# A hybrid decoder layer on one core: gate chunks of 512 columns and step sizes computed as [head, token]

## The chip, the core and the metric

The kernel runs on one core of one Trainium2 chip. The core has a matrix engine (TensorE, PE in the profile), a vector engine (VectorE, DVE), a scalar engine (ScalarE, ACT), a general engine (GpSimd, POOL) and SyncE (SP), whose queue issues all of this kernel's transfers. Each engine works through its own instructions in the order in which they stand; semaphores order them between engines. PE reads operands from the on-chip memory SBUF and writes results into PSUM; ACT and DVE read PSUM and write SBUF. The metric is the device time of one execution in microseconds (us); smaller is better.

## What is computed

One decoder layer over 256 tokens of width 1024 in float32: a SwiGLU feed-forward layer, a token mixer, a cross-attention and a second feed-forward layer, each with RMS norms. The change lies in the mixer. Its input projection gives `q`, `k`, `v` of an attention branch, `z`, `xbc` and `dt` of a state-space branch (SSD), and the logits of two gates that merge the branches:

```python
h = _rmsnorm(x, mix_pre_g)
q, k, v, z, xbc, dt_raw, gate_logits = jnp.split(h @ w_in, cuts, axis=-1)
...
dt = jax.nn.softplus(dt_raw + ssd_dt_bias)          # 32 heads, one step size per head and token
a = -jnp.exp(ssd_A_log)
y = _ssd_chunked(xh * dt[..., None], a * dt, B, C)
...
g_attn, g_ssd = jnp.split(jax.nn.sigmoid(gate_logits + b_gate), 2, axis=-1)
mixed = (g_attn * attn_out + g_ssd * ssd_out) @ w_mix_out
```

In `w_in` the 32 columns of `dt_raw` stand directly ahead of the 2048 columns of `gate_logits`.

## The kernel before

Tokens lie in two tiles of 128 (`t` = 0, 1), the width of 1024 in eight slices `k` of 128. The normalised input of the mixer is kept transposed as `hT`, a high part and a low part, both in fp32r. Every weight is loaded into a `raw` buffer (six of them) as a tile of 128 x 1024 (one slice or more), and then split: ACT copies the high part (`whi_...`), DVE subtracts it from the raw values to get the low part (`wlo_...`). There are nine slots for each part. A product is three matmuls (`mm3`, L175 to L178): high by high, high by low, low by high. The helper class `Engine` records ACT's and DVE's instructions, so they all carry the line L57 (L55 with a raised priority); they are told apart by tile names.

`proj_B` (L337) gives a product as [token, column]: the 128 tokens of tile `t` are stationary and up to 512 weight columns move. `proj_A` (L319) gives it as [column, token]: 128 weight columns are stationary and 256 tokens move. `proj_A2` (from L327, in the feed-forward layers) puts the high and the low part of `hT` side by side, so that one matmul with 512 moving columns does high by high and high by low, and a second one with 256 does low by high.

The gates and dt share one projection of 2080 columns, cut into five chunks of `GCH` = 416 (L35). `gate_w` (L652) loads and splits the weights of a chunk, four tiles of 832 columns each. `gate_chunk` (L655) does, for one token tile, 24 matmuls of 416 columns; DVE then adds the bias into `sig` (kept in two tiles, `sig0` and `sig1`) and ACT takes the tanh. In chunk 0 the first 32 columns are dt: DVE adds `dtb` and writes `dtr`.

The order of the work around it is written out by hand, and a scheduler then places each engine's instructions by that order and by priorities. Behind the last product of `v` (`da_v`, L572) come five small transposes (`cw_ps`), then gate chunk 0 for both token tiles, then a softplus of `dtr` by some twenty small DVE operations and one ACT exponential (`sp_e`, `sp_r`, `sp_u`, `sp_pl`, from L683), which end in `dt` and `adt`. Then the loop of L995 runs the attention: `q0 k0 q1 k1 q2 k2 o0 q3 o1 k3 g1 o2 g2 o3`, where `q` and `k` are projections, `o` output products, and `g1`, `g2` gate chunks. `k0` also starts `cumulate` (L703), which needs `adt`. The softmax work of the attention runs in chains that advance at fixed points (`tick`) of the projections. Behind the SSD groups come gate chunks 3 and 4 (L1024) and the merge, in which DVE multiplies and adds `sig` with the branch results (L1033 to L1038).

The splits of `q0`, `k0` and chunk 0 are told not to stand ahead of the evacuation of `hT`'s second half (`last`, L586, L677).

Of the kernel before, what the change touches and what calls it, by code (L numbers as in the profile page):

```python
# [8 lines left out]
F32 = mybir.dt.float32  # L9
# [4 lines left out]
ALU = mybir.AluOpType  # L14
# [4 lines left out]
P = 128  # L19
S = 256  # L20
NT = S // P
D = 1024
KD = D // P
# [7 lines left out]
SSD_HEADS = 32  # L31
HG = 8
HP = 64
C_Q, C_K, C_V, C_Z, C_X, C_B, C_C, C_DT = 0, 1024, 2048, 3072, 5120, 7168, 7680, 8192
GCH = 416  # L35
NSLOT = 9
WARM = 18
NRAW = 6
# [31 lines left out]
def tile_hybrid_layer(ctx: ExitStack, tc: tile.TileContext, a: dict, out: bass.AP):  # L70
    nc = tc.nc
    V, A, T, G, SY = Engine(tc, nc.vector), Engine(tc, nc.scalar), nc.tensor, nc.gpsimd, nc.sync

    cp = ctx.enter_context(tc.tile_pool(name="const", bufs=1))
    sp = ctx.enter_context(tc.tile_pool(name="small", bufs=3))
# [5 lines left out]
    def mm_bank(name):  # L81
        return ps.tile([P, 512], F32, tag="mm", bufs=2, name=name)

    def ch_bank(name):
        return ps.tile([P, 512], F32, tag="ch", bufs=2, name=name)
# [4 lines left out]
    def pool(name, bufs=1):  # L90
        return tc.tile_pool(name=name, bufs=bufs, reuse_waits="tile")
# [13 lines left out]
    def start(key, gen):  # L105
        chains[key] = gen
        active.append(key)
        step(key)
# [6 lines left out]
    def tick():  # L115
        for key in list(active):
            step(key)
# [5 lines left out]
    ident = cp.tile([P, P], F32, name="ident")  # L123
# [4 lines left out]
    def issue_after(after, i):  # L128
        return nullcontext() if after is None else tc.issue_after(after[i].ins)

    def wslot(z, name, xtra=None):
        pl, bufs, tag = (wp, NSLOT, f"w{z}") if xtra is None else xtra[z == "lo"]
        return pl.tile([P, 1024], F32R, tag=tag, bufs=bufs, name=f"w{z}_{name}")

    def wraw(name):
        return wp.tile([P, 1024], F32, tag="raw", bufs=NRAW, name=f"raw_{name}")
# [38 lines left out]
    def mm3(o, lh, ll, rh, rl, start, stop):  # L175
        T.matmul(o, lh, rh, start=start, stop=False)  # L176
        T.matmul(o, lh, rl, start=False, stop=False)  # L177
        T.matmul(o, ll, rh, start=False, stop=stop)  # L178
# [33 lines left out]
    def split_evac(bank, hi, lo, scale=1.0):  # L212
        if scale == 1.0:
            return (A.copy(hi, bank),
                    V.tensor_tensor(out=lo, in0=bank, in1=hi.bitcast(F32), op=ALU.subtract))
        return (A.activation(hi, bank, AF.Copy, scale=scale),
                V.scalar_tensor_tensor(out=lo, in0=bank, scalar=scale, in1=hi.bitcast(F32),
                                       op0=ALU.mult, op1=ALU.subtract))
# [15 lines left out]
    def hT_tiles(name):  # L234
        return parts(hp_.tile([P, KD, 2, S], F32R, tag="hT", name=f"hT_{name}"))
# [101 lines left out]
    def proj_B(w, hT, t, ks, width, bank, k0=0, first=True, last=True):  # L337
        for k in ks:
            mm3(bank, hT[0][:, k, t * P:(t + 1) * P], hT[1][:, k, t * P:(t + 1) * P], *w(k - k0, 0, width),
                first and k == ks[0], last and k == ks[-1])  # L340
            if width > 256 and k % 4 == 3 or k == KD - 1:
                tick()
# [17 lines left out]
    def cols(ap, c0, n):  # L360
        return ap[:, c0:c0 + n]
# [122 lines left out]
    mp = ctx.enter_context(tc.tile_pool(name="mix", bufs=1))  # L484
# [4 lines left out]
    w_in = a["w_in"][0]  # L489
# [62 lines left out]
    with pool("ffn1") as fp:  # L552
        steps = ffn(fp, hT1, a["ffn1_post_g"][0], w_gu, a["ffn1_w_down"][0], "f1", ws, second_tile, nrm, memory)
        hT, xns = None, []
        for t, acc_t, g_bc in steps:
            if t == 0:
                hT = hT_tiles("mx")
# [27 lines left out]
    last = []  # L585
# [4 lines left out]
    last = last[0]  # L590
# [13 lines left out]
    dtb = mp.tile([P, SSD_HEADS], F32, name="dtb")  # L604
# [35 lines left out]

    dtr = mp.tile([P, NT, SSD_HEADS], F32, name="dtr")
    b_gate = a["b_gate"][0]
    G0 = GCH - 32
    sig0 = mp.tile([P, NT, G0], F32, name="sig0")
    gctx = ExitStack()
    gpool = gctx.enter_context(tc.tile_pool(name="gates", bufs=1, side="right", reuse_waits="tile"))
    sig1 = gpool.tile([P, NT, 2 * D - G0], F32, name="sig1")

    def sig(t, c0, c1):
        return sig0[:, t, c0:c1] if c1 <= G0 else sig1[:, t, c0 - G0:c1 - G0]  # L650

    def gate_w(j, after=None):  # L652
        return Weights([cols(w_in, C_DT + j * GCH, GCH)], KD, GCH, f"gt{j}", after)

    def gate_chunk(w, j, t, bg):  # L655
        bank = mm_bank(f"gt{j}{t}")
        proj_B(w, hT, t, range(KD), GCH, bank[:, :GCH])
        g0 = max(0, j * GCH - 32)
        o = 32 if j == 0 else 0
        n = GCH - o  # L660
        if j == 0:
            V.tensor_tensor(out=dtr[:, t, :], in0=bank[:, :32], in1=dtb, op=ALU.add)
        sg = sig(t, g0, g0 + n)
        V.tensor_tensor(out=sg, in0=bank[:, o:GCH], in1=bg[:, :n], op=ALU.add)
        A.activation(sg, sg, AF.Tanh, scale=0.5)

    def gate_bias(j):
        g0 = max(0, j * GCH - 32)
        n = GCH - (32 if j == 0 else 0)
        bg = sp.tile([P, GCH], F32, tag="bg", bufs=1, name=f"bg{j}")  # L670
        with issue_after(marks["f1"], 0):
            SY.dma_start(out=bg[:, :n], in_=b_gate[g0:g0 + n].partition_broadcast(P))
        return bg


    w_g0, bg0 = gate_w(0, last), gate_bias(0)
    for t in range(NT):  # L677
        gate_chunk(w_g0, 0, t, bg0)


    W = NT * SSD_HEADS
# [16 lines left out]
    dt = mp.tile([P, NT, SSD_HEADS], F32, name="dt")  # L698
# [146 lines left out]
    def ssd_bc(dp_, g):  # L845
        wbc = Weights([cols(w_in, C_B + g * P, P), cols(w_in, C_C + g * P, P)], KD, 256, f"bc{g}")
        bcT = dp_.tile([P, 2, S], F32, tag="bcT", name=f"bcT{g}", bufs=2)
        conv(dp_, proj_A(wbc, hT, f"bc{g}"), (16 + g, 20 + g), bcT, f"b{g}")
        return bcT
# [112 lines left out]
    def ssd_ws(g):  # L962
        return [Weights([a["w_branch_ssd"][0, g * 512 + i * 256:g * 512 + (i + 1) * 256, :]], 2, D, f"ws{g}{i}")
                for i in range(2)]

    def ssd_out(g, ws, t):
        while (g, t) not in ydone:
            step(("s", g))
        y = ydone[g, t]
        for c in range(2):  # L970
            for i in range(2):
                acc_rows(sacc, ws[i], y[0], y[1], 2 * i, t, c, g == 0 and i == 0, g == 3 and i == 1)
            tick()
# [18 lines left out]
        chain_a(j)  # L992

    units = dict(q=q, k=k, g=gates, o=da_out)
    for u in "q0 k0 q1 k1 q2 k2 o0 q3 o1 k3 g1 o2 g2 o3".split():  # L995
        units[u[0]](int(u[1]))
    cs, cs_d, ecs = finish("cs")
    for t in range(NT):
        for c0, c1 in ((0, G0), (G0, 512), (512, D)):
            V.scalar_tensor_tensor(out=sig(t, c0, c1), in0=sig(t, c0, c1), scalar=1.0,  # L1000
                                   in1=acc[t][c0 // 512][:, c0 % 512:c0 % 512 + c1 - c0], op0=ALU.add, op1=ALU.mult)
    ap_ctx.close()
# [3 lines left out]
    with pool("ssd") as dp_:  # L1006
        def out_units(g):
            ws = ssd_ws(g)
            for t in range(NT):
                ssd_out(g, ws, t)  # L1010

        for g in range(4):
            bcT = ssd_bc(dp_, g)
            xsT = dp_.tile([P, 4, S], F32, tag="xsT", name=f"xsT{g}", bufs=2)
            for i in range(2):
                ssd_xs(dp_, g, i, xsT)
            w = Weights([cols(w_in, C_Z + g * 512, 512)], KD, 512, f"z{g}")
            sz = dp_.tile([P, NT, 512], F32, tag="sz", name=f"sz{g}", bufs=2)
            for t in range(NT):
                ssd_z(g, t, w, sz)  # L1020
            if g > 0:
                out_units(g - 1)
            start(("s", g), ssd_chain(dp_, g, xsT, bcT, sz))
        for j in (3, 4):  # L1024
            w, bg = gate_w(j), gate_bias(j)
            for t in range(NT):
                gate_chunk(w, j, t, bg)
        mT = hT_tiles("mg")
        ws = ssd_ws(3)
        for t in range(NT):  # L1030
            ssd_out(3, ws, t)
            with ahead(400):
                for c in range(2):  # L1033
                    mg = sig(t, D + c * 512, D + (c + 1) * 512)
                    V.scalar_tensor_tensor(out=mg, in0=mg, scalar=1.0, in1=sacc[t][c], op0=ALU.add, op1=ALU.mult)
                    for c0, c1 in ((0, G0), (G0, 512)) if c == 0 else ((512, D),):
                        mg = sig(t, D + c0, D + c1)
                        V.tensor_tensor(out=mg, in0=mg, in1=sig(t, c0, c1), op=ALU.add)  # L1038
                transpose_split(sig(t, D, 2 * D), mT[0], mT[1], t, KD, "mg", scale=0.5)

    nctx = ExitStack()
# [61 lines left out]
    hT = hT_tiles("xa")  # L1103
# [67 lines left out]
    for t in range(NT):  # L1171
# [12 lines left out]
        with ahead(400):  # L1184
            post_norm(nrm, acc[t], g_po, t, 1.0, "xa")
            xn, last = norm_tile(nrm, x_sb[:, t, :], g_pr, t, "f2", scale_on=(V, A)[t])
# [40 lines left out]
```

## Time and profile before

| | before |
|---|---|
| runs shown | 871.56, 872.61 and 1729.69 us, median 872.61 |
| profiled execution: its time | 872.02 us |
| profiled execution: span of the instructions | 870.3 us |
| mean granted TensorE clock | 0.997 of full speed |
| busy: PE, DVE, ACT | 857.5, 622.5, 500.9 us |
| chain that ended last, share of PE | 94% |

The profile is of one execution. A timeline row gives the start in us from the span's start, the time of the instruction or of a run of equal ones, the engine, the line of the kernel, the operation, output tile <- input tiles, shapes, and the count; a bracket at its end names idle time ahead of it. PE's matmuls are pipelined: one starts before the one ahead of it has ended, so their pace is read from the starts.

### The profile page before, as it was taken

The page shows a single profiled execution, that of the slowest core. Times are in us where ns is not written, and L with a number is a line of the kernel's source. Part 1 is how long each engine was busy: PE and PEld are TensorE (multiplying, and loading weights), DVE is VectorE, ACT ScalarE, POOL GpSimd, SP SyncE. Part 2 cuts the span into 40 slices and gives each one's busy share as a digit, 9 for nine tenths or more (in the row PEclk, how much of TensorE's full clock was granted, in tenths as well). Part 3 has the DMA queues.
Part 4 walks back from the last instruction along what each step waited for, and adds up shares of the span by engine and source line. Part 5 has one row for each costly group of instructions (what it writes and reads, how often), then busy time and mean ns, then how long its engine had stood idle before and what let it go on. Part 6 is the DMA issues. An engine that isn't in the chain of part 4 may idle for free.

```text
span 870.3 us, 13275 instructions
## 1 busy us (share of the span) xinstructions
PE 857.5 (99%) x4966; PEld 752.6 (86%) x4966; DVE 622.5 (72%) x1064; ACT 500.9 (58%) x867; POOL 3.7 (0%) x14
## 2 busy tenths in 40 slices
PE   8999999999999999999999999999999999999996
PEld 5888888888999999998989888899998788888885
DVE  6876556768778677897987968797574975556653
ACT  7756555645666565966775734466453754555540
POOL 0000000000000000000000000000000000000000
PEclk9999999999999999999999999999999999999998
DMA  8877667635854267656463456577452386566601
GB/s 289 286 259 248 196 200 247 203 103 160 291 145 126 88 193 252 230 152 230 144 229 139 143 177 208 179 227 253 163 181 64 120 270 214 177 201 186 191 22 49
DMA packets 117653, 161.78 MB, mean 186 GB/s; under 512 B 6452, under 2 KB 93396, under 8 KB 117076
## 3 DMA queue, kind: packets, MB, share of 16 engines
q1 hardware_dynamic: 117588, 160.93, 58.0%
q8 instruction: 39, 0.64, 0.3%
q14 instruction: 26, 0.21, 0.1%
HBM read 158.78 MB, written 2.13 MB: 185 GB/s over the span
## 4 chain that ended last, share of the span: by engine, by line
PE 94%; DVE 2%; ACT 2%; DMA 1%; issue 1%; SPq 0%; DVEq 0%; ACTq 0%
PE u_f L331 8%; PE s_f L331 8%; PE acc_f L176 5%; PE acc_f L177 5%; PE acc_f L178 5%; PE u_f L333 4%; PE s_f L333 4%; PE pA_xs L176 2%; PE pA_xs L178 2%; PE pA_xs L177 2%; PE z L176 2%; PE z L178 2%; PE z L177 2%; PE gt L176 2%; PE gt L177 2%; PE yb L915 2%
## 5 line engine op out<-in xcount | busy, mean ns | idle before, releaser
L331 PE MATMUL s_f<-hT_f,whi_f1g 128*128 128x512 f32 x160 | 40.3, 393 | 0.0
L331 PE MATMUL u_f<-hT_f,whi_f1u 128*128 128x512 f32 x160 | 40.1, 392 | 0.0
L176 PE MATMUL pA_xs<-hT_mx,whi_xs 128*128 128x256 f32 x128 | 38.8, 303 | 0.0
L57 DVE TENSOR_TENSOR wlo_f2d<-raw_f2d,whi_f2d 128x1024 fp32r<-128x1024 f32 x22 | 26.8, 1220 | 13.5 <-PE u_f L333 10.4
L178 PE MATMUL pA_xs<-hT_mx,wlo_xs 128*128 128x256 f32 x128 | 36.2, 283 | 0.0
L177 PE MATMUL pA_xs<-hT_mx,whi_xs 128*128 128x256 f32 x128 | 36.2, 283 | 0.0
L331 PE MATMUL u_f<-hT_f,whi_f2u 128*128 128x512 f32 x144 | 36.1, 392 | 0.0
L331 PE MATMUL s_f<-hT_f,whi_f2g 128*128 128x512 f32 x144 | 35.9, 391 | 0.0
L176 PE MATMUL acc_f<-whi_f1d,hh_f 128*128 128x512 f32 x88 | 35.0, 398 | 0.0
L177 PE MATMUL acc_f<-wlo_f1d,hh_f 128*128 128x512 f32 x88 | 34.9, 396 | 0.0
L178 PE MATMUL acc_f<-whi_f1d,hl_f 128*128 128x512 f32 x88 | 34.8, 396 | 0.0
L176 PE MATMUL acc_f<-whi_f2d,hh_f 128*128 128x512 f32 x88 | 34.3, 390 | 0.0
L177 PE MATMUL acc_f<-wlo_f2d,hh_f 128*128 128x512 f32 x88 | 34.3, 390 | 0.0
L178 PE MATMUL acc_f<-whi_f2d,hl_f 128*128 128x512 f32 x88 | 34.2, 389 | 0.0
L331 PEld LDWEIGHTS s_f<-hT_f,whi_f1g 128*128 128x128 f32 x160 | 29.2, 188 | 5.6
L57 DVE TENSOR_TENSOR wlo_f1d<-raw_f1d,whi_f1d 128x1024 fp32r<-128x1024 f32 x22 | 26.8, 1220 | 10.1 <-PE u_f L333 7.5
L331 PEld LDWEIGHTS u_f<-hT_f,whi_f1u 128*128 128x128 f32 x160 | 28.8, 189 | 5.2
L57 DVE TENSOR_TENSOR wlo_f1g<-raw_f1g,whi_f1g 128x1024 fp32r<-128x1024 f32 x20 | 24.3, 1218 | 11.3 <-ACT whi_f1g L57 11.3
L57 DVE TENSOR_TENSOR wlo_f2g<-raw_f2g,whi_f2g 128x1024 fp32r<-128x1024 f32 x18 | 21.9, 1221 | 13.5 <-ACT whi_f2g L57 12.6
L331 PEld LDWEIGHTS s_f<-hT_f,whi_f2g 128*128 128x128 f32 x144 | 26.3, 188 | 5.0
L57 DVE TENSOR_TENSOR wlo_f2u<-raw_f2u,whi_f2u 128x1024 fp32r<-128x1024 f32 x18 | 22.0, 1220 | 11.9 <-PE s_f L333 8.9
L331 PEld LDWEIGHTS u_f<-hT_f,whi_f2u 128*128 128x128 f32 x144 | 25.9, 189 | 4.6
(496 smaller groups left out, 2808.4 us busy)
## 6 DMA issues: line engine op xcount, KB each, us to landing
raw_f1d<-in_ffn_w_down_dram SPq DMA_DIRECT2D x22, 512.0 KB, 4.5
raw_f2d<-in_ffn_w_down_dram SPq DMA_DIRECT2D x22, 512.0 KB, 4.3
raw_f1g<-in_ffn_w_gu_dram SPq DMA_DIRECT2D x20, 512.0 KB, 5.8
raw_f1u<-in_ffn_w_gu_dram SPq DMA_DIRECT2D x20, 512.0 KB, 5.2
raw_f2g<-in_ffn_w_gu_dram SPq DMA_DIRECT2D x18, 512.0 KB, 4.6
raw_f2u<-in_ffn_w_gu_dram SPq DMA_DIRECT2D x18, 512.0 KB, 4.1
raw_gt<-in_w_in_dram SPq DMA_DIRECT2D x20, 416.0 KB, 4.0
raw_xs<-in_w_in_dram SPq DMA_DIRECT2D x16, 512.0 KB, 5.0
```

The source lines that it names most:

```text
L57: return fn(*args, **kwargs)
L176: T.matmul(o, lh, rh, start=start, stop=False)
L177: T.matmul(o, lh, rl, start=False, stop=False)
L178: T.matmul(o, ll, rh, start=False, stop=stop)
L331: T.matmul(bank, w(k, f * P, (f + 1) * P)[0], hT[2][:, k, :], start=k == 0, stop=False)
L333: T.matmul(bank[:, S:], w(k, f * P, (f + 1) * P)[1], hT[0][:, k, :], start=False, stop=k == KD - 1)
L915: T.matmul(yb[:, h * HP:(h + 1) * HP], M[:, h, :], xdt[:, h, :], start=True, stop=True)
```

## The change

The 32 dt columns leave the gate projection. The gates are cut into four chunks of 512 columns, numbered 0 to 3; a weight tile of a chunk then has 1024 columns in place of 832, and there are 16 in place of 20. No gate chunk stands ahead of `q0` any more: chunks 0 and 1 take the places of 1 and 2 in the loop, chunks 2 and 3 those of 3 and 4 behind the SSD. `sig0` and `sig1` become one tile, and the merge's additions at the cut fall away.

dt is computed apart, ahead of `q0`. Its weights (1024 x 32) come in one load of eight pieces of 32 columns (128 bytes) per partition, and are split into `whi_dt` and `wlo_dt` (256 columns). Eight matmuls with 512 moving columns (both parts of `hT`) and eight with 256 give [head, token] in one bank; ACT copies one half to `dT`, DVE adds the other, PE turns `dT` in two transposes, and DVE adds `dtb` into `dtr` for both token tiles at once. The softplus that follows is the same.

```diff
-GCH = 416
...
-    sig0 = mp.tile([P, NT, G0], F32, name="sig0")
...
     def gate_chunk(w, j, t, bg):
         bank = mm_bank(f"gt{j}{t}")
-        proj_B(w, hT, t, range(KD), GCH, bank[:, :GCH])
...
-        if j == 0:
-            V.tensor_tensor(out=dtr[:, t, :], in0=bank[:, :32], in1=dtb, op=ALU.add)
...
+        proj_B(w, hT, t, range(KD), 512, bank)
+        sg = sig(t, j * 512, (j + 1) * 512)
+        V.tensor_tensor(out=sg, in0=bank, in1=bg, op=ALU.add)
         A.activation(sg, sg, AF.Tanh, scale=0.5)
...
-    w_g0, bg0 = gate_w(0, last), gate_bias(0)
+    dt_raw = wraw("dt")[:, :KD * SSD_HEADS].rearrange("p (k f) -> p k f", k=KD)
+    SY.dma_start(out=dt_raw, in_=cols(w_in, C_DT, SSD_HEADS).rearrange("(k p) f -> p k f", p=P))
+    dt_w = [wslot(z, "dt")[:, :KD * SSD_HEADS].rearrange("p (k f) -> p k f", k=KD) for z in ("hi", "lo")]
+    split_evac(dt_raw, *dt_w)
+    db = mm_bank("dtT")
+    for k in range(KD):
+        T.matmul(db[:SSD_HEADS], dt_w[0][:, k, :], hT[2][:, k, :], start=k == 0, stop=False)
+    for k in range(KD):
+        T.matmul(db[:SSD_HEADS, S:], dt_w[1][:, k, :], hT[0][:, k, :], start=False, stop=k == KD - 1)
+    dT = wraw("dT")[:SSD_HEADS, :S]
+    A.copy(dT, db[:SSD_HEADS, S:])
+    V.tensor_tensor(out=dT, in0=db[:SSD_HEADS, :S], in1=dT, op=ALU.add)
+    tb = ch_bank("dtt")
     for t in range(NT):
-        gate_chunk(w_g0, 0, t, bg0)
+        T.transpose(tb[:, t * SSD_HEADS:(t + 1) * SSD_HEADS], dT[:, t * P:(t + 1) * P], ident[:SSD_HEADS, :SSD_HEADS])
+    V.tensor_tensor(out=dtr, in0=tb[:, :NT * SSD_HEADS].rearrange("p (t h) -> p t h", t=NT),
+                    in1=dtb.unsqueeze(1).to_broadcast([P, NT, SSD_HEADS]), op=ALU.add)
...
-    for u in "q0 k0 q1 k1 q2 k2 o0 q3 o1 k3 g1 o2 g2 o3".split():
+    for u in "q0 k0 q1 k1 q2 k2 o0 q3 o1 k3 g0 o2 g1 o3".split():
...
-        for j in (3, 4):
+        for j in (2, 3):
...
-                    for c0, c1 in ((0, G0), (G0, 512)) if c == 0 else ((512, D),):
-                        mg = sig(t, D + c0, D + c1)
-                        V.tensor_tensor(out=mg, in0=mg, in1=sig(t, c0, c1), op=ALU.add)
+                    V.tensor_tensor(out=mg, in0=mg, in1=sig(t, c * 512, (c + 1) * 512), op=ALU.add)
```

The scheduler gives ACT, DVE and PE another order. On ACT, between the evacuation of `hT`'s second half and the first weights of `q0`, there stood before (names are output <- input; `v` are copies of the `v` products, numbers are buffers):

```order
L57 CAST hT_mx<-tp_mx_2078 128x4x128
L57 CAST whi_gt_2200<-raw_gt_2198 128x832
L57 CAST whi_gt_2206<-raw_gt_2204 128x832
L57 COPY v_2025<-vb_2052 128x512
L57 CAST whi_gt_2212<-raw_gt_2210 128x832
L57 CAST whi_gt_2218<-raw_gt_2216 128x832
L57 CAST whi_q_2316<-raw_q_2314 128x1024
L57 COPY v_2024<-vb_2092 128x512
L57 CAST whi_q_2322<-raw_q_2320 128x1024
L57 CAST whi_k_2379<-raw_k_2377 128x1024
L57 CAST whi_k_2385<-raw_k_2383 128x1024
L57 COPY v_2025<-vb_2118 128x512
```

and there stands now, in the same place:

```order
L56 CAST hT_mx<-tp_mx_2078 128x4x128
L56 COPY v_2025<-vb_2052 128x512
L56 COPY v_2024<-vb_2092 128x512
L56 COPY v_2025<-vb_2118 128x512
L56 COPY raw_dT<-dtT 32x256
L56 ACT_TABLE_LOAD
L56 ACTIVATE sp_e<-sp_e 128x64
L56 CAST whi_q_2263<-raw_q_2261 128x1024
L56 CAST whi_q_2269<-raw_q_2267 128x1024
L56 CAST whi_k_2326<-raw_k_2324 128x1024
```

The casts of `q0` and `k0` stood among the copies of `v`; now they stand behind the last of these, behind the copy of the dt product and behind the softplus's exponential.

On DVE, from the splits of `q0` on, before (`cw` is the result of the five small transposes):

```order
L57 TENSOR_TENSOR wlo_q_2323<-raw_q_2320,whi_q_2322 128x1024
L57 TENSOR_TENSOR wlo_k_2380<-raw_k_2377,whi_k_2379 128x1024
L57 TENSOR_TENSOR wlo_k_2386<-raw_k_2383,whi_k_2385 128x1024
L57 TENSOR_SCALAR cw<-cw_ps 128x120
L57 TENSOR_TENSOR wlo_q_2477<-raw_q_2474,whi_q_2476 128x1024
L57 TENSOR_TENSOR dtr<-gt_2224,dtb 128x32
L57 TENSOR_TENSOR sig_2193<-gt_2224,bg_2222 128x384
L57 TENSOR_TENSOR wlo_q_2483<-raw_q_2480,whi_q_2482 128x1024
L57 TENSOR_TENSOR wlo_k_2568<-raw_k_2565,whi_k_2567 128x1024
L57 TENSOR_TENSOR dtr<-gt_2252,dtb 128x32
L57 TENSOR_TENSOR sig_2193<-gt_2252,bg_2222 128x384
L57 SCALAR_TENSOR_TENSOR sp_e<-dtr 128x64
```

and now:

```order
L56 TENSOR_SCALAR cw<-cw_ps 128x120
L56 TENSOR_TENSOR raw_dT<-dtT,raw_dT 32x256
L56 TENSOR_TENSOR dtr<-dtt,dtb 128x64
L56 SCALAR_TENSOR_TENSOR sp_e<-dtr 128x64
L56 TENSOR_SCALAR sp_r<-sp_e 128x64
L56 RECIPROCAL sp_r<-sp_r 128x64
L56 TENSOR_TENSOR sp_r<-sp_r,sp_e 128x64
L56 TENSOR_TENSOR sp_u_2234<-sp_r 128x64
L56 TENSOR_SCALAR sp_e<-dtr 128x64
L56 TENSOR_TENSOR wlo_q_2264<-raw_q_2261,whi_q_2263 128x1024
L56 TENSOR_SCALAR sp_pl<-sp_u_2234 128x64
```

The four splits of `q0` and `k0` stood ahead of `cw`; now the first of them stands behind nine operations, of which the first three wait for PE. On PE the five transposes of `cw_ps` are followed by the 16 dt matmuls, the two transposes and `q0`, with nothing between.

A third place is on DVE in the norm of the second token tile, whose result PE turns into `hT`'s second half (`pf` and `mx` are the norms behind the feed-forward layer and ahead of the mixer). Before:

```order
L57 TENSOR_TENSOR wlo_v_2021<-raw_v_2018,whi_v_2020 128x1024
L57 TENSOR_SCALAR rsy_pf_1944<-rsv_pf_1942 128x1
L57 SCALAR_TENSOR_TENSOR rsq_pf_1946<-rsy_pf_1944,rsv_pf_1942 128x1
L57 SCALAR_TENSOR_TENSOR rse_pf_1948<-rsq_pf_1946 128x1
L57 SCALAR_TENSOR_TENSOR rsl_pf_1949<-rsq_pf_1946 128x1
```

and now:

```order
L56 TENSOR_TENSOR wlo_v_2021<-raw_v_2018,whi_v_2020 128x1024
L56 TENSOR_SCALAR rsy_pf_1944<-rsv_pf_1942 128x1
L56 TENSOR_TENSOR wlo_dt<-raw_dt,whi_dt 128x256
L56 SCALAR_TENSOR_TENSOR rsq_pf_1946<-rsy_pf_1944,rsv_pf_1942 128x1
L56 SCALAR_TENSOR_TENSOR rse_pf_1948<-rsq_pf_1946 128x1
```

One operation, the split of the dt weights, has come into the chain of the norm; on ACT its partner `whi_dt` stands at the same point, ahead of the norm's sums of squares.

## Rows read from the trace of the kernel before

**Rows 1.** The page's part 4: the chain that ended last, shares of the span.
```profile
PE 94%; DVE 2%; ACT 2%; DMA 1%; issue 1%; SPq 0%; DVEq 0%; ACTq 0%
```

**Rows 2.** Timeline of PE, 219 to 250 us: start, us, instruction, shapes, count.
```profile
218.74 0.39 PE L177 MATMUL vb<-wlo_v,hT_mx 128*128 128x512 f32 x1
...
221.68 0.39 PE L178 MATMUL vb<-whi_v,hT_mx 128*128 128x512 f32 x1
...
222.42 0.46 PE L176 MATMUL gt<-whi_gt,hT_mx 128*128 128x416 f32 x1
...
231.61 0.28 PE L176 MATMUL pA_q<-hT_mx,whi_q 128*128 128x256 f32 x1
```

**Rows 3.** Timeline of ACT, 176 to 236 us.
```profile
176.14 0.37 ACT L57 COPY us_f<-u_f 128x256 f32<-128x256 f32 x1
...
204.77 0.63 ACT L57 ACTIVATE junk<-x_sb 128x512 bf16<-128x512 f32 x1 [4.59 <-DVE x_sb L57]
...
213.99 1.06 ACT L57 CAST whi_q<-raw_q 128x1024 fp32r<-128x1024 f32 x1
...
233.34 1.28 ACT L57 ACT_TABLE_LOAD   x1
234.64 0.26 ACT L57 ACTIVATE sp_e<-sp_e 128x64 f32<-128x64 f32 x1
```

**Rows 4.** Timeline of DVE, 176 to 240 us.
```profile
176.81 0.42 DVE L57 TENSOR_TENSOR u_f<-u_f,us_f 128x256 f32<-128x256 f32 x1
...
208.30 0.75 DVE L57 SCALAR_TENSOR_TENSOR xn_mx<-x_sb,rsy_mx,g_mx 128x512 f32<-128x512 f32 x1
...
215.24 1.22 DVE L57 TENSOR_TENSOR wlo_q<-raw_q,whi_q 128x1024 fp32r<-128x1024 f32 x1
...
222.59 1.22 DVE L57 TENSOR_TENSOR wlo_k<-raw_k,whi_k 128x1024 fp32r<-128x1024 f32 x1 [0.89 <-ACT whi_k L57]
...
232.38 0.22 DVE L57 SCALAR_TENSOR_TENSOR sp_e<-dtr 128x64 f32<-128x64 f32 x1
...
234.93 0.20 DVE L57 TENSOR_SCALAR sp_r<-sp_e 128x64 f32<-128x64 f32 x1
...
236.15 0.18 DVE L57 TENSOR_SCALAR sp_e<-dtr 128x64 f32<-128x64 f32 x1
```

**Rows 5.** Timeline of PE, 176 to 222 us: transposes of the second tile.
```profile
208.76 1.06 PE L224 MATMUL tp_mx<-ident,xn_mx 128*128 128x128 f32 x8
```

**Rows 6.** Chain of work that ended last, in order of time, feed-forward stage.
```profile
26.37 1.84 PE s_f L331 x8
28.21 0.95 PE s_f L333 x8
```

**Rows 7.** Timeline of SP, 160 to 260 us: transfers issued.
```profile
196.56 4.97 SPq L147 DMA_DIRECT2D raw_gt<-in_w_in_dram  x4
```

**Rows 8.** Transfers by tile: count, KB each, median us from issue to landing.
```profile
raw_q<-in_w_in_dram SPq DMA_DIRECT2D x8, 512.0 KB, 7.5
...
raw_bc<-in_w_in_dram SPq DMA_DIRECT2D x16, 256.0 KB, 4.1
...
dD<-in_ssd_D_dram SPq DMA_DIRECT2D x1, 16.0 KB, 5.1
```

**Rows 9.** Start and end: timelines of PE; a window (busy by engine, clock, DMA).
```profile
1.53 2.39 PE L503 MATMUL warm<-ident 128*128 128x128 f32 x10 [1.53 <-POOL ident masks.py:199]
...
862.71 0.39 PE L178 MATMUL acc_f<-whi_f2d,hl_f 128*128 128x512 f32 x1
...
864.00:866.00 2.00, 0.00 (x0) 0.00 (x0) 1.83 (x9) 0.00 (x0) 0.00 (x0) 0.80 0.00 0
```

**Rows 10.** Who waited for whom on PE: us in total, times, longest.
```profile
PE acc_mo L176 <- ACT hT_mg L57: 0.7, 1, 0.7
PE tp_f L224 <- DVE xn_f L57: 0.6, 1, 0.6
...
PE tp_mg L224 <- DVE sig L57: 0.4, 1, 0.4
```

## What the change should do to the time

> **What bounds the kernel now.** I read the page first, for the chain that ended last. TensorE (PE) holds 94% of it [rows 1], so a microsecond of PE work that is added or removed is a microsecond of time, and a microsecond in which PE waits is one too. The list of who waited for whom says how much of the second kind there is: behind the first 25 us PE's waits are few and short, the largest 0.7, 0.6 and 0.4 us [rows 10]. So little slack can absorb anything. Then I read the PE timeline where the change begins. The last product of `v` starts at 221.68, gate chunk 0 runs from 222.42, and at 231.61 `q0` follows without a gap [rows 2]. VectorE (DVE) shows why there is no gap: the split of `k0`'s last weights starts at 222.59 [rows 4], so every weight of `q0` and `k0` was ready some 8 us before PE asked. Chunk 0 was the cover under which ScalarE (ACT) and DVE got ahead.
>
> **The columns.** Chunk 0 took 231.61 - 222.42 = 9.19 us for its 48 matmuls of 416 columns [rows 2]; the five chunks are 240 such matmuls, 5 x 9.19 = 45.9 us. The new chunks have the shape of `v`'s products: 13 intervals between 218.74 and 221.68, 0.226 us each [rows 2], so 48 x 0.226 + 0.1 for the change of shape = 10.96, and four are 43.8. That is -2.1 us only, since a matmul costs nearly in proportion to its columns and 99,840 of them become 98,304.
>
> The step-size product is added: eight matmuls with 512 moving columns and eight with 256. The feed-forward stage issues just this pair: 1.84 and 0.95 us for eight [rows 6], so 2.8 us; that the stationary side is 32 wide and not 128 I take to change nothing, as the moving columns set the pace. Two transposes come to 0.2 (eight take 1.06 [rows 5]). Net: -2.1 + 2.8 + 0.2 = **+0.9 us**.
>
> **The wait that the change adds.** Before, `dtr` came out of chunk 0 and nobody on PE waited for it. The order shows that ACT and DVE now hold `whi_q` and `wlo_q` of `q0` behind the dt chain: ACT behind the exponential of `sp_e`, DVE behind nine operations. An engine's queue is in order, so the weights of `q0`, which lie in memory, are not split until dt is done; PE's next instructions are `q0`'s, and all of PE waits behind them. From the end E of the last dt product, with 0.05 us for each hand-over between engines:
> - ACT copies `dT`: the same 256 columns from PSUM took 0.37 [rows 3]; E + 0.42.
> - DVE adds: 0.42 for that shape [rows 4]; E + 0.9.
> - PE transposes twice, 0.25 with its drain; E + 1.2.
> - DVE `sp_e` 0.22 [rows 4] and, of the same width, `dtr`; E + 1.7.
> - ACT `exp` 0.26 (its table load of 1.28 begins at E + 0.42 and just fits [rows 3]); E + 2.0.
> - ACT `whi_q` 1.06 [rows 3]; E + 3.1. Meanwhile DVE does the five operations from `sp_r` to `sp_e`, which took 236.33 - 234.93 = 1.4 before [rows 4]; E + 3.4.
> - DVE `wlo_q` 1.22 [rows 4]; E + 4.65. The third matmul of `q0` needs it.
>
> From this I take 0.24 for two matmuls that need `whi_q` alone and the 0.25 of the transposes counted above, and add 0.16, by which a matmul's end lies behind the next one's start, and 0.25, because the second `wlo_q` comes two `sp_pl` operations and 1.22 later while PE is there after 1.4. **+4.6 us**; 3.9 if every hand-over is free, 5.3 if each is 0.15. From `k0` on the splits outrun PE again: 1.06 and 1.22 us for a tile on which PE spends 24 x 0.119 = 2.9. Without that cover each further tile would cost what it lacks.
>
> **The dt split in the norm.** DVE now does `wlo_dt` (256 columns, at most 0.42 [rows 4]) in the middle of the second tile's norm. That norm ends at 208.30 + 0.75 = 209.05 [rows 4], and PE reaches the transposes of that half at 208.76 + 0.53 = 209.3 [rows 5]: 0.2 of slack against 0.4. **+0.2**, between 0 and 0.4. `whi_dt` stands on ACT ahead of the norm's squares and waits for the dt load, which takes the place of the first gate load, at 196.56 [rows 7]. ACT does those squares at 204.77 [rows 3]. The nearest landings are 4.1 us for 256 KB in pieces of 512 bytes and 5.1 us for 16 KB in pieces of 128 bytes [rows 8]; 128 KB in pieces of 128 bytes by these lands at 201 to 202: hidden.
>
> One rule speaks against this. The Trainium skill, "DMA: Bandwidth & Descriptors", section Specifications, asks for 512 bytes or more for full rate, and says that below it a read-modify-write is made. No run here shows such a load of this size; by that rule the load would be late and the sum near the second rival's 880.6, by the landings above it is 878.8.
>
> **The clock.** PE has in those 4.9 us two transposes and two matmuls to do. The only fall of the granted clock in this trace comes at the end: the last matmul ends at 863.10 (862.71 + 0.39 [rows 9]), and a mean of 0.80 over 864 to 866 [rows 9] means half speed from 865.2 on, 2.1 us later. I take it that the clock falls here too. What the way back costs is bounded by the start: ten transposes of 128 columns took 0.24 us each [rows 9] where later ones take 0.13 [rows 5], so half pace lasted at least 2.4 us from the first one. With 2.4 to 4.5 us at half pace, half of it is lost: 1.2 to 2.2; **+1.6**. Zero if it does not fall; 2.9 if all of `q0` (48 x 0.119 = 5.7 us) is at half pace.
>
> **What comes back.** The last two chunks give DVE 2 x (10.96 - 9.19) = 3.5 us more to catch up before the merge, and the merge has one operation less for each tile. PE's waits there are 0.7 and 0.4 [rows 10]. Half of that: **-0.5**, between 0 and -1.1. Everything else moved is equal: the gate splits are 16 tiles of 1024 in place of 20 of 832, and the number of table loads stays.
>
> **Sum.** 872.0 (the profiled execution, 0.6 below the median of the runs) + 0.9 + 4.6 + 0.2 + 1.6 - 0.5 = **878.8 us**, 0.8% slower.
>
> **The rivals.**
> - *The clock holds* (chance 0.18). For: PE is not wholly idle. Against: the fall above came after less. 878.8 - 1.6 = 877.2.
> - *The dt load is late* (0.10). If it lands at 204, 7.5 us after its issue, which is the median landing of the `q` loads [rows 8], ACT's squares and DVE's norm stand behind it, and PE stops at the transposes of 208.76: up to +1.8, 880.6. It decides from a landing of about 6.5 us on.
> - *The chain is shorter than I count* (0.12): less for the hand-overs, and the merge's waits gone altogether. 875.
> - *No slower than before* (0.04): the attention stage behind `q0` is bound by its softmax chain and not by PE, so that PE, late by 6 us, finds work ready where it now waits, and is back on time. It takes 6.8 us of waits that can vanish; [rows 10] hold 1.7 us. 872 or less.
> - *Worse* (0.06): DVE, whose lead of 8 us is gone, is late for `q1`, `k1` and the softmax also. Each of the four next tiles may cost 1: 883.
>
> The likeliest, with the clock's fall, has 0.50 and lies between 876.8 and 880.8. To leave out no more than 2 in 10, and with the bounds of the terms: **874.0 to 883.0**. Over 2% (about what a measurement of this kernel can tell from no change) is 17 us, and no case comes near it: slower 0.02, faster 0.01, within 0.97.
>
> **What would show it.** In the changed profile: the 16 dt products take 2.8 us from about 222.6; then PE's largest wait of the whole program, on `wlo_q` (or `whi_q`) ahead of `q0`, whose third matmul starts near 230.5; a granted clock below 1 between 227 and 236, with intervals of 0.2 and more between `q0`'s matmuls; four gate chunks of 11 us. I am wrong if PE's wait ahead of `q0` is under 3 us or over 6, if the clock stays at 1, or if the attention stage takes longer or shorter than now by over 1.5 us.

## The result, and the profile after

| | before | after |
|---|---|---|
| median, same chip (us) | 873.25 | 879.76 |
| spread of the runs counted (us) | 871.56 to 873.54, five runs | 879.01 to 880.95, six runs |
| ratio | | 1.008, interval 1.0069 to 1.009 |
| profiled execution: its time, span (us) | 872.02, 870.3 | 879.82, 878.1 |
| mean granted clock | 0.997 | 0.996 |

The kernel became 0.8% slower, 6.5 us by the medians, as forecast (878.8 us, +6.8 on the profiled execution). One further run of the kernel before took 1729.69 us; without it the median of before is 873.2. The profiles differ by 7.8 us of span, but 1.3 of these lie ahead of anything that was changed: the first product of `v` starts at 199.23 before and at 200.52 after. They arise in the first 25 us, since from the first `s_f` of the feed-forward stage to the first of `v` it is 176.01 in both, and in the traces of the experiments the first of `v` starts anywhere from 199.27 to 201.74. The rows, of PE's timeline, start and us first, of before and then of after:

```profile
199.23 0.39 PE L176 MATMUL vb<-whi_v,hT_mx 128*128 128x512 f32 x1
```

```profile
200.52 0.39 PE L175 MATMUL vb<-whi_v,hT_mx 128*128 128x512 f32 x1
```

So stages are compared from that row on. The table is read from PE's timelines, each row from the start of one matmul to that of the next one named. "dT apart" is the first experiment below:

| stretch (us) | before | after | dT apart |
|---|---|---|---|
| first of `v` to first of `k0` | 38.12 | 38.13 | 32.39 |
| to the last of the attention's output (`acc_at`) | 103.18 | 106.63 | 106.70 |
| to the last of `z` in the SSD stage | 156.56 | 156.61 | 156.60 |
| to the first product of the merge (`acc_mo`) | 44.22 | 47.37 | 47.37 |
| to the last matmul | 321.40 | 321.28 | 321.29 |
| sum | 663.48 | 670.02 | 664.35 |

The first stretch had gate chunk 0 in it, 9.19 us, and is without it no shorter. PE stood there. The page's chain that ended last is still PE's, 95% after 94% [rows 1]:

```profile
PE 95%; ACT 2%; DVE 2%; DMA 0%; issue 0%; DVEq 0%; SPq 0%; ACTq 0%
```

but the list of who waited for whom on PE (us in total, times, longest), whose largest entries behind the start were 0.7, 0.6 and 0.4 [rows 10], now begins with three of the new place; `tp_mg`, the merge's wait of 0.4, is gone from it:

```profile
PE pA_q L175 <- ACT whi_q L56: 1.8, 1, 1.8
...
PE pA_q L177 <- DVE wlo_q L56: 1.1, 1, 1.1
PE dtt L680 <- DVE raw_dT L56: 0.9, 1, 0.9
...
PE acc_mo L175 <- ACT hT_mg L56: 0.7, 1, 0.7
```

Here is PE's timeline, to be set beside [rows 2]. A bracket names idle time ahead of a row and who ended it:

```profile
223.21 0.39 PE L177 MATMUL vb<-whi_v,hT_mx 128*128 128x512 f32 x1
...
223.94 2.02 PE L672 MATMUL dtT<-hT_mx,whi_dt 128*32 128x512 f32 x8
225.81 1.10 PE L674 MATMUL dtT<-hT_mx,wlo_dt 128*32 128x256 f32 x8
227.81 0.31 PE L680 MATMUL dtt<-ident,raw_dT 32*128 32x32 f32 x2 [0.90 <-DVE raw_dT L56]
229.91 0.39 PE L175 MATMUL pA_q<-hT_mx,whi_q 128*128 128x256 f32 x1 [1.79 <-ACT whi_q L56]
230.13 0.28 PE L176 MATMUL pA_q<-hT_mx,whi_q 128*128 128x256 f32 x1
231.55 0.38 PE L177 MATMUL pA_q<-hT_mx,wlo_q 128*128 128x256 f32 x1 [1.14 <-DVE wlo_q L56]
...
232.26 0.42 PE L175 MATMUL pA_q<-hT_mx,whi_q 128*128 128x256 f32 x1
232.48 0.41 PE L176 MATMUL pA_q<-hT_mx,whi_q 128*128 128x256 f32 x1
...
235.43 0.28 PE L175 MATMUL pA_q<-hT_mx,whi_q 128*128 128x256 f32 x1
235.54 0.28 PE L176 MATMUL pA_q<-hT_mx,whi_q 128*128 128x256 f32 x1
```

The last dt product ends at 225.81 + 1.10 = 226.91, and the third matmul of `q0` starts at 231.55, 4.64 us later. Behind it the starts are 0.21 apart instead of 0.12 until 235.4: the clock. Windows of PE's side (bounds, length, busy of PE, of its weight loads, DVE, ACT and POOL with counts, granted clock, DMA share, GB/s):

```profile
228.00:230.00 2.00, 0.21 (x3) 0.09 (x1) 1.42 (x5) 1.94 (x4) 0.00 (x0) 1.00 0.27 47
230.00:232.00 2.00, 0.86 (x5) 0.66 (x6) 1.94 (x6) 2.00 (x3) 0.00 (x0) 0.99 0.62 215
232.00:234.00 2.00, 2.00 (x12) 2.00 (x11) 1.97 (x4) 2.00 (x3) 0.00 (x0) 0.50 0.58 147
234.00:236.00 2.00, 2.00 (x13) 2.00 (x13) 1.97 (x5) 0.60 (x1) 0.00 (x0) 0.66 0.85 240
```

The chain that PE waited for is in the timelines of ACT, then of DVE, in place of [rows 3] and [rows 4]:

```profile
226.94 0.36 ACT L56 COPY raw_dT<-dtT 32x256 f32<-32x256 f32 x1 [2.73 <-PE dtT L674]
227.32 1.28 ACT L56 ACT_TABLE_LOAD   x1
228.66 0.26 ACT L56 ACTIVATE sp_e<-sp_e 128x64 f32<-128x64 f32 x1
228.83 1.98 ACT L56 CAST whi_q<-raw_q 128x1024 fp32r<-128x1024 f32 x2
```

```profile
227.34 0.41 DVE L56 TENSOR_TENSOR raw_dT<-dtT,raw_dT 32x256 f32<-32x256 f32 x1 [3.00 <-ACT raw_dT L56]
228.15 0.22 DVE L56 TENSOR_TENSOR dtr<-dtt,dtb 128x64 f32<-128x64 f32 x1 [0.40 <-PE dtt L680]
...
230.17 0.19 DVE L56 TENSOR_SCALAR sp_e<-dtr 128x64 f32<-128x64 f32 x1
230.28 1.22 DVE L56 TENSOR_TENSOR wlo_q<-raw_q,whi_q 128x1024 fp32r<-128x1024 f32 x1
```

Ahead of 226.94 ACT had stood for 2.73 us, and ahead of 227.34 DVE for 3.0. The weights of `q0` were in memory (SP issues their two loads from 201.34 on, and no load of a `q` took longer than 4.9 us to land), and neither engine reached them, since their splits stood behind the dt chain.

The dt load, which has the place of [rows 7], is issued at 197.84 and was there when ACT came to it at 201.36 without a wait; it had landed 2.5 us after its issue. Rows of SP's timeline, of ACT's, and of the transfers by tile:

```profile
197.84 0.39 SPq L667 DMA_DIRECT2D raw_dt<-in_w_in_dram  x1
```

```profile
201.36 0.40 ACT L56 CAST whi_dt<-raw_dt 128x256 fp32r<-128x256 f32 x1
```

```profile
raw_dt<-in_w_in_dram SPq DMA_DIRECT2D x1, 128.0 KB, 2.5
```

### The profile page after: what moved, and what is told of

The parts are those of the page before. It is cut to its first block, busy times and chain, and to the rows that moved or that the text cites. A ratio compares the mean times of both kernels' runs of the same rounds, so it can differ in the third digit from the quotient of the medians.

```text
span 878.1 us, 13180 instructions
## 1 busy us (share of the span) xinstructions
PE 862.3 (98%) x4936; PEld 749.2 (85%) x4936; DVE 621.4 (71%) x1055; ACT 500.3 (57%) x863; POOL 3.7 (0%) x14
## 4 chain that ended last, share of the span: by engine, by line
PE 95%; ACT 2%; DVE 2%; DMA 0%; issue 0%; DVEq 0%; SPq 0%; ACTq 0%
PE u_f L330 8%; PE s_f L330 8%; PE acc_f L175 5%; PE acc_f L177 5%; PE acc_f L176 5%; PE s_f L332 4%; PE u_f L332 4%; PE pA_xs L177 2%; PE pA_xs L175 2%; PE pA_xs L176 2%; PE gt L177 2%; PE gt L175 2%; PE acc_sd L177 2%; PE gt L176 2%; PE acc_sd L175 2%; PE z L175 2%
```

## The experiments

**1. dT apart.** One line: `dT` gets a tile of its own in place of a buffer of the `raw` ring.

```diff
-    dT = wraw("dT")[:SSD_HEADS, :S]
+    dT = mq.tile([SSD_HEADS, S], F32, name="dT")
```

> The changed kernel with one line edited: `dT` gets a tile of its own and not a buffer of the `raw` pool. In the order that results, the splits of `q0` and `k0` stand among the copies of `v` again, and the two transposes of dt stand inside `q0`. Theory 1 (queue order: the splits stood behind the dt chain only because `dT` held its place in the ring of raw buffers): PE's waits of 0.9, 1.8 and 1.1 us ahead of and inside `q0` vanish, the granted clock stays at full speed there, and the time falls by 4.5 + 1.5 = 6.0 us to 873.7, 0.5 above before. Theory 2 (cover: without gate chunk 0 ACT and DVE have no time to get ahead, wherever the splits stand): a wait of 3 us or more on `whi_q` or `wlo_q` remains, 877 or more.

Measured: 873.71 us, ratio to before 1.0011 (1.0002 to 1.002). The whole loss but 0.8 us is gone. PE's list of waits has no entry of `q0`, and in PE's timeline `q0` follows the dt product without a gap, at a pace of 0.12:

```profile
225.43 1.10 PE L674 MATMUL dtT<-hT_mx,wlo_dt 128*32 128x256 f32 x8
226.36 0.28 PE L175 MATMUL pA_q<-hT_mx,whi_q 128*128 128x256 f32 x1
...
228.15 0.28 PE L175 MATMUL pA_q<-hT_mx,whi_q 128*128 128x256 f32 x1
228.40 0.28 PE L680 MATMUL dtt<-ident,dT 32*128 32x32 f32 x2
228.61 0.39 PE L176 MATMUL pA_q<-hT_mx,whi_q 128*128 128x256 f32 x1
```

ACT splits `q0`'s first weights 17 us earlier than in the kernel after (its timeline):

```profile
211.48 1.06 ACT L56 CAST whi_q<-raw_q 128x1024 fp32r<-128x1024 f32 x1
```

So it was not chunk 0 as a cover that was missing. The product of `v` gives ACT and DVE time enough; it was the order of the splits, and the order comes from where `dT` lies. PE now turns `dT` within `q0` and waits for nobody.

**2. q0 ahead of dT.** `dT` stays in the ring, but the buffers of `q0`'s weights are taken ahead of it.

```diff
+    wq0 = Weights([cols(w_in, C_Q, 256)], KD, 256, "q0", last)
     dT = wraw("dT")[:SSD_HEADS, :S]
...
-        qb = proj_A(Weights([cols(w_in, C_Q + j * 256, 256)], KD, 256, f"q{j}", after), hT, f"q{j}")
+        w = wq0 if j == 0 else Weights([cols(w_in, C_Q + j * 256, 256)], KD, 256, f"q{j}", after)
+        qb = proj_A(w, hT, f"q{j}")
```

> The kernel after with one thing moved: the buffers of q0's weights are taken from the ring of raw buffers ahead of dT's, and dT stays in that ring. In the order the splits of q0 then stand among the copies of v again, as in the kernel before, while those of k0 stay behind the dt chain. Theory 1 (a split whose raw buffer is taken behind dT's stands behind dT's use, and that alone made the wait): no wait ahead of q0; its 48 matmuls and the transposes (6.0 us) cover k0's splits, of which the first is done 4.65 us after the last dt product and is wanted by k0's third matmul some 6.2 us after it; so no wait ahead of k0 either, the clock stays, and the time is that of e5_dT_own_tile, 873.7 us, up to 874.2 if k0 waits a little. Rival (in e5_dT_own_tile it was something else about the tile of its own that helped, such as the six raw buffers being free for loads): the wait moves from q0 to k0 or q1, of 1 us and more, and the time is 875 us or more, since dT still holds one of the six buffers until the transposes are done.

Measured: 873.86 us, ratio 1.001 (1.0 to 1.0019). The first theory holds: with `dT` in the ring as in the kernel after, the wait goes as soon as `q0`'s buffers are taken ahead of `dT`'s. The rival falls: PE's list of waits has no entry of `q0`, `k0` or `q1`, though `dT` still holds a buffer. `k0`'s splits do stay behind the dt chain on ACT and DVE, as these rows (ACT, then DVE) show:

```profile
228.16 0.36 ACT L56 COPY raw_dT<-dtT 32x256 f32<-32x256 f32 x1 [2.72 <-PE dtT L674]
...
230.14 1.99 ACT L56 CAST whi_k<-raw_k 128x1024 fp32r<-128x1024 f32 x2
```

```profile
231.59 1.22 DVE L56 TENSOR_TENSOR wlo_k<-raw_k,whi_k 128x1024 fp32r<-128x1024 f32 x1
```

but the first of them is done at 232.81, and PE works at `q0` from 227.96 to 234.13. The same chain, of the same length, costs nothing once one tile of PE's work lies in front of the splits behind it: from the first of `v` to the first of `k0` it is 32.39, as in experiment 1. The attention stage is 105.97 in this execution, 0.7 shorter than there, with PE's small products in another order; what that order is worth was not tested.

**3. The gap filled.** The kernel after, with PE kept at work in the gap.

```diff
     db = mm_bank("dtT")
...
+    fb = ch_bank("fill")
+    for _ in range(8):
+        T.transpose(fb[:, :P], ident, ident)
...
     for t in range(NT):
         T.transpose(tb[:, t * SSD_HEADS:(t + 1) * SSD_HEADS], dT[:, t * P:(t + 1) * P], ident[:SSD_HEADS, :SSD_HEADS])
+    for _ in range(15):
+        T.transpose(fb[:, :P], ident, ident)
```

> The changed kernel with 23 idle transposes of the identity on PE: nine between the dt product and its two transposes, fourteen between these and `q0`, some 1.0 and 1.5 us of work in waits of 0.9 and 1.8 us. They compute nothing that is used. Theory 1 (of the 6.5 us, 1.5 is the granted clock, which falls because PE has nothing to do): `wlo_q` is ready at the same place, some 4.65 us behind the end of the dt product, the clock stays at full speed, and the time falls by 1.3 to 1.5 us, to 878.3. Theory 2 (the clock costs nothing, the wait alone is the whole loss): 879.7 as before the edit. If the fill delays the chain: 880 or more.

Measured: 878.59 us, ratio 1.0067 (1.0053 to 1.0081). The wait for `wlo_q` stays as it was (1.1), and the clock now stays at full speed, in the two windows in which it was 0.50 and 0.66:

```profile
232.00:234.00 2.00, 2.00 (x17) 2.00 (x18) 1.97 (x5) 2.00 (x4) 0.00 (x0) 1.00 0.45 99
234.00:236.00 2.00, 2.00 (x19) 2.00 (x18) 1.97 (x4) 0.90 (x1) 0.00 (x0) 1.00 0.92 264
```

From the first of `v` to the first of `k0` it is 36.70 us in place of 38.13. That is the clock's price alone, 1.43; by the medians, each against its own before, it is 0.8 (6.51 and 5.71), which the intervals do not tell from 1.43. In these two executions experiment 3 loses 0.36 of it again behind the start of the merge (321.64 in place of 321.28); why is open. The fall was not peculiar to the profiled execution: the mean granted clock is 0.994 to 0.996 in the six runs of the kernel after, and 0.998 or 0.999 in the four runs here. What remains against "dT apart", 36.70 - 32.39 = 4.31, is the stall, over and above the turn of `dT`, which "dT apart" pays inside `q0`.

**4. dt with tokens as rows.** The product as 48 matmuls of 32 moving columns, which give [token, head] at once: no `dT`, no turn.

```diff
-    db = mm_bank("dtT")
...
+    tb = mm_bank("dtt")
     for t in range(NT):
-        T.transpose(tb[:, t * SSD_HEADS:(t + 1) * SSD_HEADS], dT[:, t * P:(t + 1) * P], ident[:SSD_HEADS, :SSD_HEADS])
+        for k in range(KD):
+            mm3(tb[:, t * SSD_HEADS:(t + 1) * SSD_HEADS], hT[0][:, k, t * P:(t + 1) * P], hT[1][:, k, t * P:(t + 1) * P],
+                dt_w[0][:, k, :], dt_w[1][:, k, :], k == 0, k == KD - 1)
```

> The changed kernel with the dt product in the form [token, head]: 48 matmuls with 32 moving columns and the tokens stationary, and DVE adds the bias from PSUM; no `dT`, no copy and no transposes. The order has `q0`'s splits among the copies of `v`. Theory 1: no wait ahead of `q0`, the clock holds; the 48 matmuls have no row yet, between 0.06 us each (2.9 us, as the columns alone would have it cheaper still) and 0.11 (5.3 us, the pace of the small 32-column matmuls of `cs_ps`); 873.8 to 876.2. Theory 2 (cover): 3 us more than that.

Measured: 878.96 us, ratio 1.0069 (1.0055 to 1.0083). A miss. There is no wait ahead of `q0`, but PE's timeline shows the pace of the 48 change in the middle:

```profile
226.33 0.26 PE L177 MATMUL dtt<-whi_dt,hT_mx 128*128 128x32 f32 x1
226.44 0.32 PE L175 MATMUL dtt<-whi_dt,hT_mx 128*128 128x32 f32 x1
226.60 0.37 PE L176 MATMUL dtt<-wlo_dt,hT_mx 128*128 128x32 f32 x1
226.81 0.37 PE L177 MATMUL dtt<-whi_dt,hT_mx 128*128 128x32 f32 x1
```

0.11 us apart up to 226.44, 0.21 behind. The windows show that it is the clock, and that PE had no gap:

```profile
224.00:226.00 2.00, 2.00 (x21) 2.00 (x20) 1.22 (x1) 0.29 (x1) 0.00 (x0) 1.00 0.97 290
226.00:228.00 2.00, 2.00 (x14) 2.00 (x13) 0.00 (x0) 0.00 (x0) 0.00 (x0) 0.63 1.08 350
228.00:230.00 2.00, 2.00 (x11) 2.00 (x11) 0.00 (x0) 0.00 (x0) 0.00 (x0) 0.50 0.96 389
```

The 48 took 7.15 us (223.07 to 230.22), of which the 18 at the slow pace are 3.8, and the beginning of `q0` ran at that pace too, so that `q0` took 7.20. At 0.111 us each the 48 would be 5.3, and `q0` takes 5.74 in the kernel before: the fall cost some 1.8 + 1.5 = 3.3 us, more than the 2.8 by which the run lies above the upper end of what was expected.

**5. The same 48, mixed with q0.** Three of them stand behind each three of `q0`'s.

```diff
...
+    for f in range(2):
+        for k in range(KD):
+            mm3(qv0[:, f, :], *wq0(k, f * P, (f + 1) * P), hT[0][:, k, :], hT[1][:, k, :], k == 0, k == KD - 1)
+            mm3(tb[:, f * SSD_HEADS:(f + 1) * SSD_HEADS], hT[0][:, k, f * P:(f + 1) * P], hT[1][:, k, f * P:(f + 1) * P],
+                dt_w[0][:, k, :], dt_w[1][:, k, :], k == 0, k == KD - 1)
...
```

> The same 48 matmuls of 32 moving columns as e4_dt_token_rows, but three of them stand behind each three matmuls of q0's product (256 moving columns), in place of all 48 in a row ahead of it. Theory A (in e4_dt_token_rows the granted clock fell because TensorE had nothing but 32-column matmuls for over 3 us): mixed with q0's the clock stays at full, the 48 cost 48 x 0.111 = 5.3 us against 3.1 for the product and the transposes of e5_dT_own_tile, so 873.71 + 2.2 = 875.9 us, and q0 with the 48 takes 48 x 0.119 + 5.3 = 11.0 us. Theory B (matmuls of 32 columns lower the clock in any company, or the fall came from something else at that time, as the splits of ACT and DVE): the clock falls to half between 226 and 236 again and costs 2.5 to 3.5 us as it did there: 878.5 to 879.5. Either way no wait ahead of q0; dtr comes some 4 us later than in e4_dt_token_rows, and if cumulate's matmuls then wait for it, that shows as a wait of TensorE for adt and comes on top.

Measured: 876.43 us, ratio 1.0037 (1.0023 to 1.0051). The clock stays at 1.00 in every window from 222 to 238, of which two:

```profile
226.00:228.00 2.00, 2.00 (x19) 2.00 (x18) 0.00 (x0) 0.00 (x0) 0.00 (x0) 1.00 1.08 392
228.00:230.00 2.00, 2.00 (x20) 2.00 (x19) 0.00 (x0) 0.00 (x0) 0.00 (x0) 1.00 0.89 352
```

`q0` with the 48 takes 11.1 us (11.0 expected). Theory B falls, and theory A's forecast holds: the same matmuls, with DMA about as busy (0.89 to 1.08) and with ACT and DVE as idle from 226 to 230 as in experiment 4, leave the clock alone in the company of longer ones. The time is 0.5 over its 875.9; 0.3 of that is the chip, on which the kernel before takes 873.16 in place of 872.88, and the attention stage is 0.3 longer, 107.02 us in place of 106.70.

**6. One pass, turned by a product.** "dT apart", with the high and the low part of the dt weights side by side as 64 stationary columns, so that the second eight matmuls go; the two halves are added in the turn, by matmuls against two identities on top of each other (`sel`). The dt split, besides, is told to stand behind the evacuation of `hT`'s second half.

```diff
-    split_evac(dt_raw, *dt_w)
...
+    with tc.issue_after(last[0].ins):
+        split_evac(dt_raw, dt_w[:, :, 0, :], dt_w[:, :, 1, :])
...
-    for k in range(KD):
-        T.matmul(db[:SSD_HEADS], dt_w[0][:, k, :], hT[2][:, k, :], start=k == 0, stop=False)
-    for k in range(KD):
-        T.matmul(db[:SSD_HEADS, S:], dt_w[1][:, k, :], hT[0][:, k, :], start=False, stop=k == KD - 1)
+    for k in range(KD):
+        T.matmul(db[:H2], dt_w[:, k, :], hT[2][:, k, :], start=k == 0, stop=k == KD - 1)
...
-        T.transpose(tb[:, t * SSD_HEADS:(t + 1) * SSD_HEADS], dT[:, t * P:(t + 1) * P], ident[:SSD_HEADS, :SSD_HEADS])
+        T.matmul(tb[:, t * SSD_HEADS:(t + 1) * SSD_HEADS], dT[:, t * P:(t + 1) * P], sel, start=True, stop=True)
```

> The one-line edit of `dT`, and the high and the low part of the dt weights side by side as 64 stationary columns: one pass of eight matmuls with 512 moving columns in place of eight with 512 and eight with 256; the two transposes become matmuls with two stacked identities, which also add the two halves; the dt split is told to stand behind the evacuation of `hT`'s second half, out of the norm. Theory 1: 0.95 us less on PE than with the one-line edit and 0.2 less in the norm: 872.6, 0.6 below before. If PE's pace went by the stationary columns too, the product would take over 1.84 us and the gain would be less than 0.5.

Measured: 874.14 us, ratio 1.0016 (1.0007 to 1.0025). A miss: no gain over "dT apart".

**7. One pass, turned by transposes.** As 6, without `sel`; the edit is shown against 6.

```diff
-        T.matmul(tb[:, t * SSD_HEADS:(t + 1) * SSD_HEADS], dT[:, t * P:(t + 1) * P], sel, start=True, stop=True)
+        T.transpose(tb[:, t * H2:(t + 1) * H2], dT[:, t * P:(t + 1) * P], ident[:H2, :H2])
...
+    V.tensor_tensor(out=dtr, in0=tv[:, :, SSD_HEADS:], in1=dtr, op=ALU.add)
```

> As e7_one_pass (dT in a tile of its own; the high and the low part of the dt weights side by side as 64 stationary columns, one pass of eight matmuls with 512 moving columns), but [head, token] is turned by two transposes of 64 rows, as the kernel after does with 32, and DVE adds the two halves in the operation that follows; there is no matmul against a stacked identity and no tile for it. TensorE then has eight matmuls at 0.23 us (1.9 us) and two transposes (0.3 us) for dt, against 16 matmuls (2.8 us), two transposes (0.3) and 0.2 in the norm in e5_dT_own_tile. Theory 1 (a microsecond taken off TensorE here is a microsecond of time, and what e7_one_pass gave back later came from the stacked identity): 873.71 - 0.9 - 0.2 = 872.6 us, the feed-forward stage ahead of it and the attention stage behind it as long as in e5_dT_own_tile. Theory 2 (the gain is given back whatever the turn is, in the attention stage behind q0, or because the dt split now stands ahead of q0's): 873.7 to 874.2, with the attention stage 0.3 us or more longer than in e5_dT_own_tile.

Measured: 873.04 us beside 873.16 for the kernel before, ratio 1.0 (0.9991 to 1.0009): level with it, and 0.4 over what theory 1 gave, of which 0.3 is again the chip. Product and turn in PE's timelines of 6 and then of 7:

```profile
223.46 2.05 PE L679 MATMUL dtT<-hT_mx,whi_dt 128*64 128x512 f32 x8
...
226.76 0.63 PE L685 MATMUL dtt<-sel,dT 64*128 64x32 f32 x4
```

```profile
224.16 2.06 PE L675 MATMUL dtT<-hT_mx,whi_dt 128*64 128x512 f32 x8
...
227.61 0.33 PE L681 MATMUL dtt<-ident,dT 64*128 64x64 f32 x2
```

The product is 0.9 shorter than in "dT apart" in both. In 6 the turn takes 0.63 where transposes take 0.33, and two stretches that have no part in the edit are longer: from the first `s_f` of the feed-forward stage to the first of `v` 176.28 us (175.99 in "dT apart", 176.01 in 7), and the attention 107.14 (106.70, and 106.77 in 7). The medians do not decide between the theories of 7: that of "dT apart" is from another chip, and the interval of 7 reaches 0.8 us to either side. The stretches speak for theory 1: from the first of `v` to the last matmul it is 663.50 in 7 against 664.35 in "dT apart", and the attention stage is not 0.3 longer. What 6 loses goes with `sel` and its matmuls, the turn aside; how a tile of 32 columns does that was not tested.

## Why the prediction was right

**The wait ahead of q0, +4.6.** The place, the chain that PE waits for and the price were as forecast. The steps, from the end of the last dt product: copy done at +0.39 (forecast 0.42), addition +0.84 (0.9), turn +1.21 (1.2), exponential +2.01 (2.0), DVE free for `wlo_q` +3.37 (3.4), `wlo_q` done +4.59 (4.65), third matmul of `q0` at +4.64. The price of the stall, from experiments 3 and 1, is 4.3, and 4.76 with the turn of `dT` (0.45, below), which in the kernel after lies inside the stall; the forecast has 4.6 + 0.2 for the two. The 0.25 which I had added for the second `wlo_q` was too much: in experiment 3, at full clock, it is 0.06 (233.39 to 233.57 between two starts that are 0.12 apart elsewhere), and in the kernel after the slowed clock had PE arrive later still.

I named the order as the cause and called the chunk that went "the cover". Experiment 1 corrects the second half: even without the cover there is no stall when the splits stand among the copies of `v`. The prediction read the order and did not ask what made it; experiments 1 and 2 show that it was the place of `dT` in the ring.

**The clock, +1.6.** Measured 1.43 in the profile, 0.8 by the medians; in both below the 1.6. It fell, but later than in the one fall that the prediction had to go by: 2.1 us behind PE's last work there, here only at some 232, when PE was working again, 5 us behind the last dt product. It lasted 3.4 us. That this lies within the 2.4 to 4.5 taken from the start is luck as far as the rows go: the ten transposes there were slow, but the windows of the kernel before give a granted clock of 1.00 for them, so that the rows do not show the start as a stretch at half clock.

```profile
2.00:4.00 2.00, 1.92 (x9) 1.52 (x8) 0.00 (x0) 0.44 (x2) 0.29 (x1) 1.00 0.87 286
```

The other factor, that half of such a stretch is lost, was a little too large: the starts are 0.214 apart in place of 0.12 (232.04 to 235.04 for 14 of them), and 44% of 3.4 us is 1.5.

**The columns and the product, +0.9.** Sixteen dt products take 2.8 us in "dT apart" (from 223.56 to `q0`'s start at 226.36), as forecast. Of the gate chunks two made the attention stage 3.45 longer; the two behind the SSD are the same work, so 6.9 came for the 9.19 that went: -2.3, forecast -2.1. The turn is the term that was too small: `q0` takes 6.19 us with it in "dT apart" and 5.74 before, 0.45 where I had put 0.2. Two transposes put into another product also cost the changes of shape: 228.15, 228.40, 228.61 are 0.25 and 0.21 apart where 0.12 is the pace. With it the term is -2.3 + 2.8 + 0.45 = +0.95.

**The split in the norm, +0.2.** From the first to the last of `v` it is 22.45 before and 22.69 after: +0.24, and the norm's end moved with it. In experiments 6 and 7, where the split stands behind the norm, this is all but gone (22.51 and 22.46).

**What comes back, -0.5.** The wait of `tp_mg` is gone, and the stretch ahead of the merge grew by 3.15 where two chunks make 3.45: -0.3, within the 0 to -1.1 of the forecast.

Sum of what was measured: 0.95 + 4.3 + 0.24 + 1.43 - 0.3 = 6.6, against 6.8 forecast and 6.5 by the medians. The forecast's 878.8 stands 1.0 below the median of after, because it was made against the profiled execution of 872.0, and the medians of before on the chips used since are 872.9 to 873.3.

**The rivals.** "The clock holds" fell with the windows above; experiment 3 shows what it would have been worth. "The chain is shorter than I count" fell: the third matmul of `q0` starts at +4.64, where the count has +4.65 for its weights. "The dt load is late" fell: 128 KB in pieces of 128 bytes landed 2.5 us after the issue, quicker than the landings of [rows 8], so the sum by the landings was right. The Trainium skill, "DMA: Bandwidth & Descriptors", section Specifications, asks for 512 bytes or more for full rate; for one load of this size this trace shows no price of it on the path. "No slower than before" fell: the attention stage behind `k0` is 3.45 longer, as its two longer chunks make it, and takes nothing back. "Worse" fell: behind `q0` there is no wait of `k0` or `q1`.

## What to carry to other kernels

A small tile that is the result of a product should not be taken from the ring through which the weights stream: what is loaded into buffers taken behind it stood behind its use on ACT, DVE and PE here, and that cost 5.7 us of stall and clock, which one line gave back. Before a wait is put down to lost cover, ask what fixes the order in which the waiting engine does its work, and move just that. And a small product with narrow moving columns is not free in proportion: what it costs is seen in its pace beside the same weights' other products, and in the clock behind it.

## What the runs showed of the hardware that I had not expected

The granted clock fell to half (1.2 of 2.4 GHz) at 226.5 in experiment 4 while PE issued matmuls of 32 moving columns without a gap, busy 2.00 of 2.00 us; with three of 256 columns between each three of them (experiment 5) it did not. In the kernel after it fell once PE had begun again, not during its waits. What decides between these I can't tell from these runs.

A matmul of 32 moving columns against 128 x 128 weights took 0.111 us at full clock, barely less than the 0.12 of one with 256 columns. And two float32 matmuls against a plain matrix stood in the trace as four, with 0.63 us, where two transposes of the same operand took 0.33.
